# Second block's attentions: two heads of a pair issued side by side, zero-padded remainders of k, and a larger share of projections before the last two groups' suffix sums

## The chip, the core and the metric

The kernel runs on one NeuronCore of a Trainium2 chip. The engines are TensorE (PE, matrix products, with PEld for its weight loads), VectorE (DVE), ScalarE (ACT), GpSimd (POOL) and SyncE (SP, which issues DMAs). The metric is the device time of one execution in microseconds (us): 3792.46 us before, the median of 3 runs (3791.65 to 3796.62).

## The reference, cut to what matters

Two transformer blocks over 512 tokens of width 1024, each with two layers. The change touches only the second block's token mixing, which has three branches per layer, eight heads of 64 values each:

```
for l in range(2):
    h = rmsnorm(x); proj = h @ w_in[l]          # gates, q, k, v of three branches
    y_a = causal_softmax_attention(q_a, k_a, v, 96 ** -0.5)       # "MLA", q and k 96 wide
    y_b = stick_breaking_attention(sb_q, sb_k, sb_v)               # q and k 64 wide
    y_c = silu(r_g) * head_group_norm(retention(r_q, r_k, r_v))    # q and k 64 wide
    x = x + sum_n(sigmoid(gate_n) * (y_n @ w_branch[l, n])) @ w_out[l]
    x = x + square(relu(rmsnorm(x) @ w_up[l])) @ w_down[l]

# stick breaking, per block of 128 keys and the queries at or after them:
z = q @ k.T / 8
between = reverse_cumsum(log_sigmoid(-z)) - log_sigmoid(-z)      # suffix sums over keys
a = where(key < query, exp(log_sigmoid(z) + between), 0);  y = a @ v
```

## The kernel before, in words

All operands are float32. A projection keeps its precision by splitting weight and activation into a rounded part and a remainder and multiplying three times per 128 rows of contraction (`mm3`, lines 330, 332 and 334; `vproj`, lines 1197 to 1199, for the values). These products have 512 (or 256) columns and go through TensorE in one pass. Products of attention weights with values are plain float32; the trace counts two records for each.

`mix` (one call per layer) runs three attentions, each woven with projections: `weave(main, filler)` takes steps of the attention, and after each step issues as many products of the next projections as the number that the step yields (`FILL`, an estimate in us). TensorE works in the order in which it is given instructions; a scheduler orders the other engines' instructions around it.

**MLA** (`mla`). A block is one head and 128 queries. Step i issues the scores of block i (three products, lines 1352 to 1354), then softmax on VectorE and ScalarE, the transposes of block i-2 (line 1370), and the products with v of block i-3 (`mla_av`, line 1382). A head's output takes 64 of the 128 output rows of the array: head 0 of a pair writes rows 0 to 63 of the PSUM tile `yp`, head 1 rows 64 to 127. Blocks run head by head, so neighbouring products write the same half.

**Stick breaking** (`stick`). Eight heads times three groups of key blocks, (2,3), (1) and (0), make 24 groups. Step i issues the scores of group i (`dots`, lines 1323 and 1324), then a chain over VectorE (1428), ScalarE (exp, ln), VectorE (1432), GpSimd (mask, 1437) and VectorE (1439, 1440) that leaves softplus split into two tiles; the suffix sums of group i-2 (`sb_sums`, line 1449), which add to the same PSUM tile; and after a head's third group its products with v (`sb_av`, `av`, line 1291).

**Retention** (`retention`). Two heads of a pair and one key block per step: four score products (lines 1548 and 1550), a product with the decay on VectorE, and the products with v of the step before, which alternate between the two heads already.

For the scores of stick breaking and retention, `pairs` splits q and k into rounded part and remainder. One product over all 128 rows of contraction takes [k rounded; k rounded] with [q rounded; q remainder]; a second, over the 64 rows of the head alone, adds k's remainder times q rounded:

```
nc.tensor.matmul(o, kk[e][:, S], qq[e][:, s * P:], ...)
nc.tensor.matmul(o, kl[half[e], S], qq[e][half[e], s * P:], ...)
```

Tiles come from pools with a fixed number of buffers of 128x512: `ta` (TA = 12) holds attention tiles, `th` (TH = 9) rounded parts and remainders. A new tile waits until an old one is no longer read. In the first block, the neighbourhood attention (`mix` of `na`, line 1000) already issues the products of two heads alternately.

Of the kernel before, what the change touches and what calls it, by code (L numbers as in the profile page):

```python
# [8 lines left out]
F32 = mybir.dt.float32  # L9
F32R = mybir.dt.float32r  # L10
# [3 lines left out]
ALU = mybir.AluOpType  # L14
# [3 lines left out]
P = 128  # L18
# [42 lines left out]
T2 = 16  # L61
TA = 12
TH = 9
TY = 10
NAF = (1.2, 0.55)
NAE = 0.35
FILL = (0.9, 1.9, 1.2)
# [190 lines left out]
class Net:  # L258
# [897 lines left out]
    def mix(self, l, x, xd, xh, xl, pool):  # L1156
# [91 lines left out]
        nc.vector.tensor_tensor(out=t1[64:128], in0=t1[64:128], in1=tk[64:128], op=ALU.add)  # L1248
        kk = []
        for i in range(2):  # L1250
            kh, kl = th(), th()
            self.split(kh[64:128], kl[64:128], t1[64:128])
            kk.append((kh, kl))
        rkv = ta()
# [51 lines left out]

        def pairs(raw):
            q, k = raw
            qq, kk, kl = [th(), th()], [th(), th()], th()
            for e, R in enumerate(half):  # L1310
                nc.scalar.activation(out=qq[e][R], in_=q[R], func=AF.Copy)
                nc.scalar.activation(out=kk[e][R], in_=k[R], func=AF.Copy)
            for e, R in enumerate(half):
                O = half[1 - e]
                nc.vector.tensor_tensor(out=qq[e][O], in0=q[R], in1=qq[e][R].bitcast(F32), op=ALU.subtract)
                nc.vector.tensor_copy(kk[e][O], kk[e][R].bitcast(F32))
                nc.vector.tensor_tensor(out=kl[R], in0=k[R], in1=kk[e][R].bitcast(F32), op=ALU.subtract)
            return qq, kk, kl

        def dots(o, h, s, qk, start):  # L1320
            e, S = h % 2, slice(s * P, s * P + P)
            qq, kk, kl = qk
            nc.tensor.matmul(o, kk[e][:, S], qq[e][:, s * P:], start=start, stop=False, skip_group_check=True)
            nc.tensor.matmul(o, kl[half[e], S], qq[e][half[e], s * P:], start=False, stop=True, skip_group_check=True)

        def next_pair(raw, p):
            if p < 4:
                live["qk", p] = pairs(raw[p])

# [5 lines left out]
        ya = []  # L1335
        blocks = [(h, b) for h in range(8) for b in range(4)]
        live = {}

        def mla_scores(h, b):
            e = h % 2  # L1340
            if b == 0:
                qh, ql = th(), th()
                nc.scalar.activation(out=qh, in_=qraw[h], func=AF.Copy)
                nc.gpsimd.tensor_tensor(out=ql, in0=qraw[h], in1=qh.bitcast(F32), op=ALU.subtract)
                kh, kl = kk[e]
                self.split(kh[:64], kl[:64], kraw[h // 2][64 * e:64 * e + 64])
                live["q"] = (qh, ql)
            (qh, ql), (kh, kl) = live["q"], kk[e]
            w = (b + 1) * P
# [24 lines left out]

        def mla_av(h, b):
            e = h % 2
            if e == 0 and b == 0:
                live["yp"] = yps()
            yp, T = live["yp"], live.pop((h, b))
            c0 = 64 * (h % 4)  # L1380
            for c in range(b + 1):
                nc.tensor.matmul(yp[64 * e:64 * e + 64, b * P:b * P + P], vm[h // 4][:, c, c0:c0 + 64],
                                 T[:, c * P:c * P + P], start=(c == 0), stop=(c == b), skip_group_check=True)
            if e == 1 and b == 3:
                ya.append(out_pair(yp))

        def mla():
            n = len(blocks)
            for i in range(n + 3):
                if i < n:  # L1390
                    mla_scores(*blocks[i])
                    yield FILL[0]
                if 0 <= i - 2 < n:
                    mla_tr(*blocks[i - 2])
                    yield FILL[0]
                if 0 <= i - 3 < n:
                    mla_av(*blocks[i - 3])
                    yield FILL[0]
            for i in range(4):
                self.tap(f"ya{i}", ya[i][0].bitcast(F32))  # L1400
# [13 lines left out]

        self.exp_ln()
        yb = []

# [38 lines left out]

        def sb_av(g):
            h = g["h"]
            p, e = h // 2, h % 2
            if e == 0:  # L1460
                live["yp"] = yps()
            for s in range(4):
                av(live["yp"], e, sv, h, g["a"][s], s)
            if e == 1:
                yb.append(out_pair(live["yp"]))
                self.tap(f"yb{p}", yb[p][0].bitcast(F32))

        def stick():
            groups = []
            next_pair(sb, 0)  # L1470
            for i in range(24 + 3):
                if i < 24:
# [6 lines left out]
                    if h % 2 and j == 0:  # L1479
                        next_pair(sb, h // 2 + 1)  # L1480
                    yield FILL[1]
                if 0 <= i - 2 < 24:
                    sb_sums(groups[i - 2])
                    yield FILL[1]
                if 0 <= i - 3 < 24 and (i - 3) % 3 == 2:
                    sb_av(groups[i - 3])
                    yield FILL[1]

# [46 lines left out]
        def ret_scores(p, s):  # L1535
# [13 lines left out]
            for e, z in enumerate(zs):  # L1549
                nc.tensor.matmul(z, kl[half[e], S], qq[e][half[e], s * P:], start=False, stop=True)  # L1550
            if s == 0:
# [258 lines left out]
```

## Time and profile before

| what | value |
|---|---|
| median of 3 runs | 3792.46 us |
| profiled execution, its own time | 3786.87 us |
| its span, first to last instruction | 3785.1 us |
| mean granted TensorE clock | 0.995 of full speed |
| PE busy | 3717.2 us (98%), 19776 instructions |
| PEld busy | 3011.1 us (80%) |
| DVE busy | 2087.4 us (55%) |
| ACT busy | 1424.6 us (38%) |
| POOL busy | 357.6 us (9%) |

A matmul's recorded duration is longer than what it costs in a stream, since one is in the array while the next enters. What an instruction costs TensorE is read from starts: the start of the next instruction less its own. In layer 0 the MLA stage runs from about 1921 to 2065 us of the span, stick breaking to about 2240, retention from 2252 to 2323; layer 1 repeats them some 960 us later.

### The profile page before, as it was taken

To read this page: it belongs to the slowest core of one execution; us is meant where nothing else is said; L and a number is where in the kernel's file an instruction comes from. 1 tells how busy PE (TensorE), PEld (TensorE's weight loads), DVE (VectorE), ACT (ScalarE), POOL (GpSimd) and SP (SyncE) were. 2 spreads that over 40 slices of the span, in tenths; PEclk is the share of its full clock that TensorE was granted. 3 is DMA by queue.
4 is the path that set the end of the run, shared out by engine and by line. 5 is a ranking of instruction groups with operands and counts; after the bars stand their busy time and mean duration, and the time that the engine had idled before them with its cause. 6 is when DMAs were issued, how large, how long until landed. Compare 5 with 4: busy or idle time off the path is not lost. (4 is left out here: it accounts for less than half of the span.)

```text
span 3785.1 us, 49321 instructions
## 1 busy us (share of the span) xinstructions
PE 3717.2 (98%) x19776; PEld 3011.1 (80%) x19776; DVE 2087.4 (55%) x3320; ACT 1424.6 (38%) x2183; POOL 357.6 (9%) x334
## 2 busy tenths in 40 slices
PE   7999999999999998999999999999999999999998
PEld 6777778888878886888787777888888777688888
DVE  5556653333356775444855775455455576655446
ACT  4333432122344544333545434322234543433223
POOL 2000000000001110000300111211020012112001
PEclk9999999999999999999999999999999999999999
DMA  6343442222222122333322222333332212233333
GB/s 248 126 128 125 140 139 62 62 65 64 62 64 57 50 58 73 95 96 98 111 74 62 67 89 78 118 99 95 101 117 73 65 58 89 80 121 95 100 95 117
DMA packets 122020, 351.86 MB, mean 93 GB/s; under 512 B 30896, under 2 KB 33200, under 8 KB 121792
## 3 DMA queue, kind: packets, MB, share of 16 engines
q1 hardware_dynamic: 87648, 309.11, 26.0%
q10 hardware_dynamic: 32000, 31.67, 2.9%
q0 software_dynamic: 2144, 7.93, 0.5%
q8 instruction: 156, 2.56, 0.3%
q14 instruction: 72, 0.59, 0.0%
HBM read 333.71 MB, written 8.65 MB: 90 GB/s over the span
## 5 line engine op out<-in xcount | busy, mean ns | idle before, releaser
L319 ACT ACTIVATE whi<-wst 128x1024 fp32r<-128x1024 f32 (+3 forms) x503 | 527.3, 1049 | 1404.8 <-PE mm L332 1197.2
L320 DVE TENSOR_TENSOR wlo<-wst,whi 128x1024 fp32r<-128x1024 f32 (+3 forms) x503 | 671.0, 1334 | 330.0 <-ACT whi L319 324.1
L330 PE MATMUL mm<-xh,whi 128*128 128x512 f32 x1664 | 672.0, 404 | 6.0 <-ACT xh L472 3.0
L332 PE MATMUL mm<-xl,whi 128*128 128x512 f32 x1664 | 652.6, 392 | 0.2
L334 PE MATMUL mm<-xh,wlo 128*128 128x512 f32 x1664 | 651.0, 391 | 0.0
L330 PEld LDWEIGHTS mm<-xh,whi 128*128 128x128 f32 x1664 | 313.3, 188 | 90.8 <-issue 26.4
L330 PE MATMUL mm<-ty,whi 128*128 128x512 f32 (+1 forms) x1008 | 382.8, 380 | 0.1
L334 PE MATMUL mm<-ty,wlo 128*128 128x512 f32 (+1 forms) x1008 | 378.9, 376 | 0.0
L334 PEld LDWEIGHTS mm<-xh,wlo 128*128 128x128 f32 x1664 | 313.3, 188 | 69.6 <-issue 2.6
L332 PEld LDWEIGHTS mm<-xl,whi 128*128 128x128 f32 x1664 | 313.9, 189 | 60.3 <-issue 2.3
L330 PE MATMUL mm<-hh,whi 128*128 128x256 f32 (+2 forms) x1176 | 339.5, 352 | 6.4 <-ACT hh L482 2.2
L332 PE MATMUL mm<-hl,whi 128*128 128x512 f32 (+2 forms) x1176 | 332.3, 345 | 2.0 <-DVE hl L486 1.5
L334 PE MATMUL mm<-hh,wlo 128*128 128x512 f32 (+2 forms) x1176 | 329.0, 343 | 0.5 <-DVE wlo L320 0.5
L332 PE MATMUL mm<-ta,whi 128*128 128x512 f32 (+1 forms) x752 | 279.0, 371 | 0.4 <-DVE ta L325 0.4
L330 PEld LDWEIGHTS mm<-hh,whi 128*128 128x128 f32 (+1 forms) x1176 | 188.3, 188 | 65.8 <-issue 34.2
L330 PEld LDWEIGHTS mm<-ty,whi 128*128 128x128 f32 x1008 | 189.7, 188 | 40.6 <-issue 6.2
L334 PEld LDWEIGHTS mm<-ty,wlo 128*128 128x128 f32 x1008 | 189.7, 188 | 35.6 <-issue 1.0
L332 PEld LDWEIGHTS mm<-hl,whi 128*128 128x128 f32 (+1 forms) x1176 | 189.0, 188 | 28.8 <-DVE hl L486 2.0
L334 PEld LDWEIGHTS mm<-hh,wlo 128*128 128x128 f32 (+1 forms) x1176 | 188.5, 188 | 28.9 <-DVE wlo L320 1.0
L332 PEld LDWEIGHTS mm<-ta,whi 128*128 128x128 f32 x752 | 141.7, 188 | 24.9 <-DVE ta L325 0.6
L827 DVE SCALAR_TENSOR_TENSOR x<-mm,mod,x 128x512 f32<-128x512 f32 x52 | 39.0, 750 | 182.2 <-PE mm L334 182.2
L1636 DVE TENSOR_TENSOR x<-x,mm 128x512 f32<-128x512 f32 x56 | 38.5, 687 | 172.1 <-PE mm L334 172.1
(418 smaller groups left out, 6060.3 us busy)
## 6 DMA issues: line engine op xcount, KB each, us to landing
wst<-w_in SPq DMA_DIRECT2D x100, 512.0 KB, 3.5
wst<-ffn_in SPq DMA_DIRECT2D x88, 512.0 KB, 3.5
aw<-ada_w SPq DMA_DIRECT2D x72, 512.0 KB, 4.3
wst<-w_dn SPq DMA_DIRECT2D x70, 512.0 KB, 3.5
wst<-w_up SPq DMA_DIRECT2D x64, 512.0 KB, 3.5
wst<-ffn_out SPq DMA_DIRECT2D x32, 448.0 KB, 3.2
wst<-w_br SPq DMA_DIRECT2D x24, 512.0 KB, 3.5
wst<-gla_qkr SPq DMA_DIRECT2D x16, 512.0 KB, 3.8
```

The lines of the kernel that those rows point to most:

```text
L319: nc.scalar.activation(out=hi[:, :n], in_=st[:, :n], func=AF.Copy)
L320: nc.vector.tensor_tensor(out=lo[:, :n], in0=st[:, :n], in1=hi[:, :n].bitcast(F32), op=ALU.subtract)
L330: nc.tensor.matmul(o, whi, xh, start=first, stop=False)
L332: nc.tensor.matmul(o, whi, xl, start=False, stop=False)
L334: self.after = nc.tensor.matmul(o, wlo, xh, start=False, stop=last)
L827: nc.vector.scalar_tensor_tensor(out=x[:, n, a:b], in0=o[:, :b - a], scalar=gsc, in1=x[:, n, a:b], op0=ALU.mult, op1=ALU.add)
L1636: nc.vector.tensor_tensor(out=x[:, n, :], in0=x[:, n, :], in1=o, op=ALU.add)
```

## The change

1. MLA's blocks are ordered by pair: (pair, query block, head). The products with v wait until both heads' blocks are transposed and are issued for both, alternating between the two halves of `yp`. The q parts of both heads are held at once.
2. Stick breaking's products with v are issued per pair of heads, after the sixth group, alternating in the same way.
3. The remainder of k goes into a tile of four that live on (`kz`), whose other 64 rows hold zeros, written once per layer by GpSimd. The second score product of stick breaking and retention now runs over all 128 rows. MLA's own k tiles use the same four buffers before.
4. Steps 24 and 25 of stick breaking, which have no scores to issue, yield 4.0 each to the projections, ahead of the suffix sums of groups 22 and 23.
5. TA from 12 to 15, TH from 9 to 8.

```diff
-TA = 12
-TH = 9
+TA = 15
+TH = 8
...
-        kk = []
-        for i in range(2):
-            kh, kl = th(), th()
+        kz = [tag("kz", 4, F32R) for _ in range(4)]
+        kk = [kz[0:2], kz[2:4]]
+        for kh, kl in kk:
             self.split(kh[64:128], kl[64:128], t1[64:128])
...
-        def pairs(raw):
+        def pairs(raw, par):
-            qq, kk, kl = [th(), th()], [th(), th()], th()
+            qq, kk, kl = [th(), th()], [th(), th()], kz[2 * par:2 * par + 2]
...
-                nc.vector.tensor_tensor(out=kl[R], in0=k[R], in1=kk[e][R].bitcast(F32), op=ALU.subtract)
+                nc.vector.tensor_tensor(out=kl[e][R], in0=k[R], in1=kk[e][R].bitcast(F32), op=ALU.subtract)
...
-            nc.tensor.matmul(o, kl[half[e], S], qq[e][half[e], s * P:], start=False, stop=True, skip_group_check=True)
+            nc.tensor.matmul(o, kl[e][:, S], qq[e][:, s * P:], start=False, stop=True, skip_group_check=True)
...
-        blocks = [(h, b) for h in range(8) for b in range(4)]
+        blocks = [(2 * p + e, b) for p in range(4) for b in range(4) for e in range(2)]
...
-        def mla_av(h, b):
+        def mla_av(p, b):
+            yp, Ts = live["yp"], [live.pop((2 * p + e, b)) for e in range(2)]
             for c in range(b + 1):
+                for e, T in enumerate(Ts):
+                    c0 = 64 * (2 * p % 4 + e)
+                    nc.tensor.matmul(yp[64 * e:64 * e + 64, b * P:b * P + P], vm[p // 2][:, c, c0:c0 + 64],
+                                     T[:, c * P:c * P + P], start=(c == 0), stop=(c == b), skip_group_check=True)
...
-                if 0 <= i - 3 < n:
-                    mla_av(*blocks[i - 3])
-                    yield FILL[0]
+                if i >= 4 and i % 2 == 0:
+                    mla_av(blocks[i - 4][0] // 2, blocks[i - 4][1])
+                    yield 2 * FILL[0]
...
+        for i, z in enumerate(kz):
+            nc.gpsimd.memset(z[half[1 - i % 2]].bitcast(F32), 0.0)
...
+        def sb_av(p, gs):
+            yp = yps()
             for s in range(4):
+                for e, g in enumerate(gs):
+                    av(yp, e, sv, 2 * p + e, g["a"][s], s)
...
+                elif i < 26:
+                    yield 4.0
...
-                if 0 <= i - 3 < 24 and (i - 3) % 3 == 2:
-                    sb_av(groups[i - 3])
-                    yield FILL[1]
+                if 0 <= i - 3 < 24 and (i - 3) % 6 == 5:
+                    sb_av((i - 3) // 6, (groups[i - 6], groups[i - 3]))
+                    yield 2 * FILL[1]
...
-                nc.tensor.matmul(z, kl[half[e], S], qq[e][half[e], s * P:], start=False, stop=True)
+                nc.tensor.matmul(z, kl[e][:, S], qq[e][:, s * P:], start=False, stop=True)
```

How this moves TensorE's instructions, at two places. First, in MLA of layer 0 before the change, a block's products with v (line 1382, here one key block of one head) between projections (lines 330, 332, 334), with the scores of the next block (1352 to 1354) behind:

```order
L334 MATMUL mm<-xh,wlo 128x512
L1382 MATMUL yp<-ta,v 64x128
L330 MATMUL mm<-xh,whi 128x512
L332 MATMUL mm<-xl,whi 128x512
L334 MATMUL mm<-xh,wlo 128x512
L330 MATMUL mm<-xh,whi 128x512
L332 MATMUL mm<-xl,whi 128x512
L334 MATMUL mm<-xh,wlo 128x512
L1352 MATMUL ma<-th 128x128
```

The same stage after the change, where the line is 1381 and x4 counts two key blocks of two heads:

```order
L1381 MATMUL yp<-ta,v 64x128 x4
L330 MATMUL mm<-xh,whi 128x512
L332 MATMUL mm<-xl,whi 128x512
L334 MATMUL mm<-xh,wlo 128x512
L330 MATMUL mm<-xh,whi 128x512
L332 MATMUL mm<-xl,whi 128x512
L334 MATMUL mm<-xh,wlo 128x512
L330 MATMUL mm<-xh,whi 128x512
L332 MATMUL mm<-xl,whi 128x512
L334 MATMUL mm<-xh,wlo 128x512
L1351 MATMUL ma<-kz,th 128x512
```

The products with v stand in half as many places, each with both heads' products and more projections behind it. Second, TensorE in stick breaking of layer 0 before the change: one head's products with v (line 1291), one per key block:

```order
L334 MATMUL mm<-ty,wlo 128x512
L1291 MATMUL yp<-ta,v 64x512
L1291 MATMUL yp<-ta,v 64x384
L1291 MATMUL yp<-ta,v 64x256
L1291 MATMUL yp<-ta,v 64x128
L330 MATMUL mm<-ty,whi 128x512
```

After the change (line 1290):

```order
L334 MATMUL mm<-ty,wlo 128x512
L1290 MATMUL yp<-ta,v 64x512 x2
L1290 MATMUL yp<-ta,v 64x384 x2
L1290 MATMUL yp<-ta,v 64x256 x2
L1290 MATMUL yp<-ta,v 64x128 x2
L330 MATMUL mm<-ty,whi 128x512
```

Both heads' products now stand at one place, alternating, at the end of the pair; the place at the end of the first head is gone.

## Rows read from the trace of the kernel before

**Rows 1.** Windows, layer 0's MLA and stick breaking: us, busy PE, PEld, DVE, ACT, POOL, clock, DMA
```profile
1921.00:2065.00 144.00, 144.00 (x823) 115.35 (x821) 78.99 (x211) 70.79 (x152) 8.41 (x6) 1.00 0.20 63
2065.00:2240.00 175.00, 174.88 (x865) 134.40 (x865) 125.12 (x232) 74.15 (x121) 26.55 (x38) 1.00 0.24 73
```

**Rows 2.** Timeline, PE, MLA: start us, us, engine, line, operation, tiles
```profile
1961.31 1.09 PE L1382 MATMUL yp<-ta,v 128*64 128x128 f32 x8
1962.33 0.50 PE L1352 MATMUL ma<-th 128*128 128x512 f32 x1
...
1994.11 0.40 PE L334 MATMUL mm<-xh,wlo 128*128 128x512 f32 x1
1994.43 0.87 PE L1382 MATMUL yp<-ta,v 128*64 128x128 f32 x6
1995.23 0.50 PE L330 MATMUL mm<-xh,whi 128*128 128x512 f32 x1
1995.57 0.40 PE L332 MATMUL mm<-xl,whi 128*128 128x512 f32 x1
1995.81 0.39 PE L334 MATMUL mm<-xh,wlo 128*128 128x512 f32 x1
```

**Rows 3.** Timeline, PE and PEld, first block's neighbourhood attention, heads alternating
```profile
1200.59 1.09 PE L1000 MATMUL po<-T,v 128*64 128x128 f32 x16
1201.61 0.39 PE L924 MATMUL mm<-whi,hh 128*128 128x256 f32 x1
...
1200.59 0.85 PEld L1000 LDWEIGHTS po<-T,v 128*64 128x64 f32 x16
```

**Rows 4.** Timeline, PE, stick breaking, one head's products with v
```profile
2094.94 2.37 PE L1291 MATMUL yp<-ta,v 128*64 128x512 f32 x8
2097.23 0.50 PE L330 MATMUL mm<-ty,whi 128*128 128x512 f32 x1
```

**Rows 5.** Timeline, PE, retention, two heads' products with v
```profile
2257.14 1.08 PE L1291 MATMUL yp<-ta,v 128*64 128x512 f32 x4
2258.15 0.50 PE L330 MATMUL mm<-xh,whi 128*128 128x512 f32 x1
```

**Rows 6.** Timeline, PE, stick breaking, first score product and next projection, groups (0), (2,3)
```profile
2071.21 0.40 PE L1323 MATMUL ma<-th 128*128 128x512 f32 x1
...
2071.96 0.50 PE L330 MATMUL mm<-xh,whi 128*128 128x512 f32 x1
...
2099.42 0.28 PE L1323 MATMUL ma<-th 128*128 128x256 f32 x1
...
2100.45 0.50 PE L330 MATMUL mm<-ty,whi 128*128 128x512 f32 x1
```

**Rows 7.** Timeline, PE, retention, first of four score products and next projection
```profile
2252.27 0.62 PE L1548 MATMUL ma<-th 128*128 128x512 f32 x2
...
2253.24 0.50 PE L330 MATMUL mm<-xh,whi 128*128 128x512 f32 x1
```

**Rows 8.** Timeline, stick breaking: chain of group 0; split and sums of groups 21, 23
```profile
2065.09 0.56 DVE L1428 TENSOR_SCALAR ta<-ma 128x384 uint32<-128x384 uint32 x1 [0.23 <-PE ma L1324]
...
2071.57 0.56 DVE L1440 TENSOR_TENSOR ta<-ta 128x384 fp32r<-128x384 f32 x1
...
2074.13 0.80 PE L1449 MATMUL ma<-ta,rc 128*128 128x128 f32 x6
...
2220.14 0.56 DVE L1440 TENSOR_TENSOR ta<-ta 128x384 fp32r<-128x384 f32 x1
...
2225.99 0.80 PE L1449 MATMUL ma<-ta,rc 128*128 128x128 f32 x6
...
2233.66 0.68 DVE L1440 TENSOR_TENSOR ta<-ta 128x512 fp32r<-128x512 f32 x1
...
2236.20 1.37 PE L1449 MATMUL ma<-ta,rc 128*128 128x512 f32 x8
```

More of the change, by code (lines that the diff above doesn't have):

```diff
@@ L1248, in mix @@
         nc.vector.tensor_tensor(out=t1[64:128], in0=t1[64:128], in1=tk[64:128], op=ALU.add)
-        kk = []
-        for i in range(2):
-            kh, kl = th(), th()
+        kz = [tag("kz", 4, F32R) for _ in range(4)]
+        kk = [kz[0:2], kz[2:4]]
+        for kh, kl in kk:
             self.split(kh[64:128], kl[64:128], t1[64:128])
-            kk.append((kh, kl))
         rkv = ta()
@@ L1323, in dots @@
             nc.tensor.matmul(o, kk[e][:, S], qq[e][:, s * P:], start=start, stop=False, skip_group_check=True)
-            nc.tensor.matmul(o, kl[half[e], S], qq[e][half[e], s * P:], start=False, stop=True, skip_group_check=True)
+            nc.tensor.matmul(o, kl[e][:, S], qq[e][:, s * P:], start=False, stop=True, skip_group_check=True)
         def next_pair(raw, p):
             if p < 4:
-                live["qk", p] = pairs(raw[p])
+                live["qk", p] = pairs(raw[p], p % 2)
         def out_pair(src):
@@ L1346, in mla_scores @@
                 self.split(kh[:64], kl[:64], kraw[h // 2][64 * e:64 * e + 64])
-                live["q"] = (qh, ql)
-            (qh, ql), (kh, kl) = live["q"], kk[e]
+                live["q", e] = (qh, ql)
+            (qh, ql), (kh, kl) = live["q", e], kk[e]
             w = (b + 1) * P
@@ L1373, in mla_tr @@
             live[h, b] = T
-        def mla_av(h, b):
-            e = h % 2
-            if e == 0 and b == 0:
+        def mla_av(p, b):
+            if b == 0:
                 live["yp"] = yps()
-            yp, T = live["yp"], live.pop((h, b))
-            c0 = 64 * (h % 4)
+            yp, Ts = live["yp"], [live.pop((2 * p + e, b)) for e in range(2)]
             for c in range(b + 1):
-                nc.tensor.matmul(yp[64 * e:64 * e + 64, b * P:b * P + P], vm[h // 4][:, c, c0:c0 + 64],
-                                 T[:, c * P:c * P + P], start=(c == 0), stop=(c == b), skip_group_check=True)
-            if e == 1 and b == 3:
+                for e, T in enumerate(Ts):
+                    c0 = 64 * (2 * p % 4 + e)
+                    nc.tensor.matmul(yp[64 * e:64 * e + 64, b * P:b * P + P], vm[p // 2][:, c, c0:c0 + 64],
+                                     T[:, c * P:c * P + P], start=(c == 0), stop=(c == b), skip_group_check=True)
+            if b == 3:
                 ya.append(out_pair(yp))
@@ L1388, in mla @@
             n = len(blocks)
-            for i in range(n + 3):
+            for i in range(n + 4):
                 if i < n:
@@ L1455, in sb_sums @@
                 g["a"][s] = l1[:, o:o + NL - s * P]
[L1457 to L1461, printed above, removed]
+        def sb_av(p, gs):
+            yp = yps()
             for s in range(4):
[L1463 to L1466, printed above, removed]
+                for e, g in enumerate(gs):
+                    av(yp, e, sv, 2 * p + e, g["a"][s], s)
+            yb.append(out_pair(yp))
+            self.tap(f"yb{p}", yb[p][0].bitcast(F32))
         def stick():
```

## The prediction

> **What bounds the kernel now.** I read the profile in this order: the table of busy shares, the busy time of each engine in the stages that change, then TensorE's timeline from start to start around every kind of product that the change touches, and last how long before the suffix sums their operands are ready. In both stages of [rows 1] TensorE is busy for the whole window (144.00 of 144 us, 174.88 of 175) at the full clock, the 2.4 GHz level, so what a product costs TensorE is what it costs the kernel. VectorE is the next engine, with 125.12 of 175 us in stick breaking.
>
> The second thing to see is that some products cost far more than their columns. A projection product of 512 columns starts 0.24 us before the next (1995.57 to 1995.81) [rows 2]; I use 0.23, the step that repeats through the stage within 0.01. The products with v fill half of the array's output rows. Three of them, for one head, take 0.80 us (1994.43 to 1995.23), four take 1.02 (1961.31 to 1962.33): 0.22 each and 0.14 once per burst [rows 2]. Going in costs 0.09 more (0.32 instead of 0.23 ahead of 1994.43), coming out 0.11 more (0.34 instead of 0.23 after 1995.23) [rows 2]. So a burst of n products costs 0.22 n + 0.34.
>
> **Term 1, MLA's products with v, -28.5 us.** Two layers, eight heads and four blocks make 64 bursts with 160 products: 160 x 0.22 + 64 x 0.34 = 57.0 us. The change pairs the products of two heads, which write different halves. What a pair costs is shown by the first block's neighbourhood attention, which already alternates: 16 records, eight products, take 1.02 us (1200.59 to 1201.61) [rows 3], what four take for one head. So 80 pairs in 32 bursts cost 80 x 0.22 + 32 x 0.34 = 28.5.
>
> A rule speaks against this. The Trainium skill ("TensorE: Matmul & The Clock Gate", Part 3, on packing small matmuls) lets a weight load run beside a product in flight only where the two use different row groups; both heads here use all rows, so each load would stand in line with the other head's product. The trace disagrees: with the 16 loads busy for 0.85 us, the whole burst of [rows 3] lasts only 1.02. By the row term 1 is 28.5 us, by the rule it is 10.9 (second rival).
>
> **Term 2, stick breaking's products with v, -19.6.** One head's four products, of 512 to 128 columns, take 2.29 us [rows 4], with 0.20 in and out 2.49; 16 heads cost 39.8. Two heads' products of 512 columns, alternating in retention, take 1.01 (2257.14 to 2258.15) [rows 5]; less the 0.14 per burst that is 0.87 per 512 columns. A pair's 1280 columns cost 0.87 x 2.5 + 0.14 + 0.20 = 2.52, eight pairs 20.2.
>
> **Term 3, stick breaking's scores, -23.0.** Each product over the half array sits between two over the whole one, and each turn costs. Group (0) takes 0.75 us for two products of 512 columns (2071.21 to 2071.96), and 0.10 on coming out [rows 6]; two whole-array products of that width take 0.46 [rows 2]. Gain 0.39. Group (2,3) takes 1.03 for four (2099.42 to 2100.45) and 0.11 [rows 6]; at half the width or less, four cost at most 4 x 0.12, by half of the 0.23. Gain 0.66. Group (1), with one turn like (0), I take at 0.39. That is 1.44 per head, 23.0 for 16. No row shows the zero-padded product itself; the bounds are the price of a whole-array product and, if the padding gained nothing, zero.
>
> **Term 4, retention's scores, -6.** Two whole and two half products of 512 columns take 0.97 us (2252.27 to 2253.24) [rows 7] and 0.10 out; four whole ones 0.92. Gain 0.15, over 32 steps 4.8. The narrower three widths pay the same turns on less work, but two heads share a turn, so the 0.39 of term 3 (12.5 us) is the other end. I take 6, near its own row. Products with v alternate there already and stay.
>
> **Sum on TensorE:** 28.5 + 19.6 + 23.0 + 6 = 77.1 us.
>
> **What it may cost.** In stick breaking the chain of a group hides behind the projections between its scores and its sums. Group 0's splits end at 2071.57 + 0.56 = 2072.13 and its sums start at 2074.13, 2.0 us later; group 21's are 5.3 ahead (2220.70 to 2225.99), group 23's 1.9 (2234.34 to 2236.20) [rows 8]. Between a group's scores and its sums TensorE now saves about 0.4 to 0.7 us for each score group passed. The first groups lose up to half of their 2.0 us, so I allow 1 us per layer: 2 us; bounds zero and 4 (the whole 2.0 per layer). The last two get the 2 x 4.0 us of projections that ran after them: group 23 gains cover, and what stands ahead of retention shrinks by as much. That costs nothing if the first retention pair is split in time; its q and k are projected long before. If that cover were too short, the nearest row for such a chain is 7.0 us (2065.09 to 2072.13) [rows 8] per layer, 14 in all.
>
> MLA's k tiles are now rewritten after the last block of one pair for the first of the next, where there used to be another head's four blocks between. The PE order leaves projections, transposes and a v burst in between, which I count as enough: zero; the nearest row for a late operand, 2.0 us [rows 8], times six turns is 12. The four memsets of GpSimd per layer wait for MLA's last scores; behind them in its queue stands only the mask of group 0. VectorE's subtraction into `kz` needs no free `th` tile any more, so a small gain is possible too: zero, within 2 us either way. The same holds for the scheduler's other choices with 15 and 8 tiles. The number of VectorE, ScalarE and DMA instructions in these stages stays, but for the memsets and the split of which tile takes them.
>
> So the change is 77.1 - 2 = 75 us. The profiled execution lasts 3786.87 us (span 3785.1 and 1.8 around it), and would come to 3712; the median of the runs is 5.6 above it, and the same step from 3792.46 gives **3717 us**.
>
> **Rivals.**
> - *VectorE becomes the bound of stick breaking.* For: it is busy 125.12 of 175 us [rows 1], and terms 2 and 3 take 21 us per layer out of the window, which brings it to 81%, in order and with waits. Against: its results lie 5.3 us ahead of the sums late in the stage [rows 8], more than the first groups have. Price: if VectorE gets no faster at all, TensorE gains only that lead, 5.3 of 21.3 us per layer; 32 us are lost: 3749.
> - *The pairs don't overlap* (the change doesn't do what it says; the rule of the skill named above would bring this about). MLA then costs 160 x 0.22 + 32 x 0.34 = 46.1 instead of 57.0, a gain of 10.9; stick breaking eight bursts of 2 x 2.15 + 0.34 = 4.64, 37.1 instead of 39.8. Terms 1 and 2 give 13.6 instead of 48.1: 3752. Against: [rows 3, 5] show the overlap, once with one bank and 128 columns, once with the same `yp` tile.
> - *Slower, by the `ta` tiles.* A pair's six tiles of weights now live until both heads are done, so up to nine such tiles and six split tiles are held: all 15. If the first group of the next pair finds no tile until the pair's products with v have run, its whole chain, 7.0 us [rows 8], and the wait for the burst ahead stand open at each of eight pair turns. From 9.4 us per turn the 75 are gone; at 9.9 it is 3796. Against: 12 tiles were as tight (six and six) at every head, and TensorE lost nothing there.
> - *Cover gone at stage boundaries* (the 14 and 12 us above): 3731 to 3743.
>
> **How the numbers follow.** Forecast 0.80, by itself 3708 to 3727 (term 4 up to 12.5 and a gain of 2 with waits of 1; or waits of 12). VectorE as the bound 0.09, boundaries 0.05, no overlap 0.03, slower 0.03. The range 3708 to 3738 holds the forecast and part of the boundary and VectorE cases; below 2 in 10 is left out. Within 0.2% (7.6 us, what a measurement of this kernel can tell from no change) no case has its centre; I give 0.02 for mixtures of the last three. Faster 0.95, slower 0.03.
>
> **What would show it right or wrong.** In the profile after: bursts of MLA's products with v at 0.36 to 1.02 us for two heads; one pair's products in stick breaking at about 2.3 us; steps of 0.23 us for both score products at 512 columns, without a long one behind; both stages with TensorE still busy throughout; stick breaking about 21 us and MLA about 14 us shorter per layer. It is wrong if TensorE's timeline shows holes ahead of the suffix sums or the transposes, if VectorE's share in stick breaking goes over 90%, or if a pair's burst takes 4 us.

## The result, and the profile after

The changed kernel takes 3752.39 us (median of 4 runs, 3751.86 to 3753.64) beside 3792.06 us for the kernel before in the same comparison: a ratio of 0.9897, 95% interval 0.9884 to 0.9909. That is 40 us faster. The forecast was 75 us, and 3752 lies 14 us above the top of its range. The profiled execution lasts 3752.21 us, its span 3750.4.

Three windows of the changed kernel in layer 0 answer to [rows 1]: MLA, the stick breaking from its first score product to the last suffix sums, and from there to retention's first score product. The columns are those of [rows 1].

```profile
1925.20:2054.10 128.90, 127.87 (x803) 106.03 (x801) 76.91 (x210) 69.42 (x149) 7.51 (x8) 1.00 0.22 69
2054.10:2215.70 161.60, 158.90 (x876) 133.62 (x876) 119.27 (x225) 73.35 (x123) 27.37 (x38) 0.99 0.25 75
2215.70:2238.20 22.50, 14.19 (x52) 9.20 (x52) 10.96 (x17) 2.14 (x3) 3.59 (x2) 0.77 0.31 94
```

MLA is shorter and nearly full. The stick breaking's last stretch is neither: TensorE is busy 14.19 of 22.50 us at a granted clock of 0.77. The same stretches, from TensorE's starts in layer 0 of each kernel's profile (us; "last sums" is the first product of group 23's sums, and retention is from its first to its last score product; the other kernels are those of the experiments below):

| kernel | MLA | stick breaking to last sums | to retention | sum of the two | retention |
|---|---|---|---|---|---|
| before | 140.9 | 172.3 | 16.1 | 188.4 | 65.7 |
| after | 128.9 | 161.6 | 22.5 | 184.1 | 63.2 |
| mla_pair_only | 128.2 | 172.1 | 16.1 | 188.2 | 65.9 |
| sb_pair_only | 140.9 | 165.3 | 20.1 | 185.4 | 65.7 |
| kz_only | 141.1 | 164.3 | 17.5 | 181.8 | 63.2 |
| yield_only | 140.9 | 180.5 | 11.8 | 192.3 | 65.7 |
| no_yield | 128.9 | 160.2 | 20.3 | 180.5 | 63.3 |
| rg_last | 128.9 | 164.4 | 17.3 | 181.7 | 63.3 |
| exch_out | 128.9 | 157.1 | 9.9 | 167.0 | 63.2 |
| exch_sp | 128.9 | 157.1 | 15.6 | 172.7 | 63.2 |
| exch_sp_rot_pool | 128.9 | 158.1 | 12.0 | 170.1 | 63.2 |
| early_act | 128.9 | 170.4 | 9.9 | 180.3 | 63.2 |

MLA gave 12.0 us a layer and retention 2.5. The stick breaking gave only 4.3, of 21 expected. Layer 1 reads alike (12.0, 2.5 and 3.6). Over both layers that is 36.9 us; the spans of the two profiled executions differ by 34.7.

TensorE's timeline of the changed kernel, answering [rows 2, 4, 6, 7]: MLA's four products for each of two heads (x16) and what follows; a pair's products in stick breaking; the scores of a group (2,3); retention's first scores.

```profile
1959.76 1.09 PE L1381 MATMUL yp<-ta,v 128*64 128x128 f32 x16
1960.79 0.39 PE L1197 MATMUL mm<-whi,xh 128*128 128x256 f32 x1
...
2182.41 2.38 PE L1290 MATMUL yp<-ta,v 128*64 128x512 f32 x16
2184.72 0.50 PE L330 MATMUL mm<-xh,whi 128*128 128x512 f32 x1
...
2188.24 0.28 PE L1322 MATMUL ma<-th 128*128 128x256 f32 x1
...
2188.65 0.45 PE L330 MATMUL mm<-xh,whi 128*128 128x512 f32 x1
...
2238.24 0.62 PE L1548 MATMUL ma<-th 128*128 128x512 f32 x2
...
2239.16 0.40 PE L330 MATMUL mm<-xh,whi 128*128 128x512 f32 x1
```

So the products cost what was forecast: 1.03 us for two heads' four products in MLA (1.02), 2.31 for a pair in stick breaking (2.32), 0.41 for the four of a group (2,3) (at most 0.48), 0.92 for retention's four (0.92).

What went wrong stands at the end of the stage. TensorE, from group 23's sums (L1450) to the last pair's products with v (L1290):

```profile
2215.75 1.76 PE L1450 MATMUL ma<-ta,rc 128*128 128x512 f32 x8
2217.34 0.44 PE L330 MATMUL mm<-xh,whi 128*128 128x512 f32 x1
...
2219.56 1.07 PE L1290 MATMUL yp<-ta,v 128*64 128x512 f32 x2
2228.82 4.53 PE L1290 MATMUL yp<-ta,v 128*64 128x512 f32 x14 [8.19 <-DVE ta L1455]
2233.28 0.80 PE L330 MATMUL mm<-xh,whi 128*128 128x512 f32 x1
```

The pair's burst lasts from 2219.56 to 2233.28, 13.72 us in place of 2.31. It waits 8.19 us for VectorE's L1455, the masking of the last weights. ScalarE and VectorE in the same time (ACTq is ScalarE's issue of transfers):

```profile
2220.24 2.46 ACTq L1514 DMA_DIRECT2D tf<-s  x4
2222.81 0.60 ACT L301 ACTIVATE ta<-ma 128x512 f32<-128x512 f32 x1 [8.71 <-DMA tf<-s]
```
```profile
2215.52 0.68 DVE L1441 TENSOR_TENSOR ta<-ta 128x512 fp32r<-128x512 f32 x1
...
2219.53 0.68 DVE L1207 TENSOR_TENSOR s<-mm,rsb 128x512 f32<-128x512 f32 x1
...
2226.01 0.69 DVE L1516 TENSOR_TENSOR s<-s,cosr 128x512 f32<-128x512 f32 x1 [4.67 <-DMA tf<-s]
2227.86 0.69 DVE L1517 TENSOR_TENSOR s<-s,tf 128x512 f32<-128x512 f32 x1 [1.15 <-POOL tf L1515]
2228.47 0.29 DVE L1455 COPY_PREDICATED ta<-rc,con_mask_sb 128x128 f32<-128x128 uint32 x1
```

Read it in order. Group 23's second split (L1441) ends at 2216.20, when its sums have begun at 2215.75: the lead of 1.9 us in [rows 8] is gone, and that alone costs little. The sums are through at 2217.34, so its exponential (L301, from `ma`) could start then. But ahead of it in ScalarE's queue stand four copies of retention's rotary step (L1514, the exchange of 32-row blocks), and these wait for the tile that VectorE's L1207 scales, finished at 2220.21. They are issued from 2220.24 for 2.46 us, and only then, 5.5 us late, the exponential runs. It ends at 2223.41. Now L1455 stands in VectorE's queue behind L1516, which waits for those copies to land, and L1517, which waits for GpSimd: 2228.47, another 5.1 us late. None of these rotary instructions belongs to the work that TensorE waits for.

The clock makes it worse. The granted clock around the hole is the figure behind the five engines' busy times:

```profile
2219.50:2228.80 9.30, 1.13 (x3) 0.19 (x2) 3.47 (x7) 1.54 (x2) 1.77 (x1) 0.78 0.41 137
2228.80:2233.30 4.50, 4.48 (x15) 2.36 (x15) 1.68 (x2) 0.00 (x0) 0.00 (x0) 0.50 0.49 127
2233.30:2238.20 4.90, 4.90 (x19) 4.03 (x19) 2.08 (x3) 0.60 (x1) 1.81 (x1) 0.84 0.13 49
```

After the idle stretch the remaining seven products run wholly at 0.50, the 1.2 GHz level: 4.46 us (2228.82 to 2233.28) for what takes about 1.9 at the full one (an estimate: the whole pair's 2.31 less one of two 512-column products, 0.87 / 2). The same queueing makes a smaller hole earlier in the stage. ScalarE's exponential of another group's sums waits 1.45 us for a copy's issue, so the PSUM tile that the next scores want comes free late, and the next 5 us have a granted clock of 0.68:

```profile
2174.79 0.49 ACT L301 ACTIVATE ta<-ma 128x384 f32<-128x384 f32 x1 [1.45 <-DMA tf<-s]
```
```profile
2175.34 0.50 PE L1322 MATMUL ma<-th 128*128 128x512 f32 x1 [1.90 <-ACT ta L301]
```
```profile
2175.00:2180.00 5.00, 4.66 (x17) 3.94 (x17) 2.27 (x5) 1.75 (x3) 1.67 (x1) 0.68 0.32 113
```

TensorE's whole list of waits names both, over two layers (total, times, longest); neither line is in that of before:

```profile
PE yp L1290 <- DVE ta L1455: 16.6, 2, 8.4
...
PE ma L1322 <- ACT ta L301: 4.5, 4, 1.9
```

### The profile page after: what moved, and what is told of

Read it like the earlier page. It is cut to its first block, busy times and chain, and to the rows that moved or that the text cites. A ratio compares the mean times of both kernels' runs of the same rounds, so it can differ in the third digit from the quotient of the medians.

```text
span 3750.4 us, 49324 instructions
## 1 busy us (share of the span) xinstructions
PE 3655.5 (97%) x19776; PEld 2996.6 (80%) x19776; DVE 2074.2 (55%) x3320; ACT 1421.1 (38%) x2183; POOL 365.0 (10%) x342
## 4 chain that ended last, share of the span: by engine, by line
PE 43%; DVE 3%; DMA 2%; ACT 1%; POOL 1%; issue 1%; ACTq 0%; DVEq 0%; POOLq 0%; SPq 0%
PE mm L330 12%; PE mm L334 12%; PE mm L332 12%; DMA tf<-s 1%; PE yp L1290 1%; PE mm L1197 1%; PE mm L1199 1%; PE mm L1198 1%; PE ma L1450 1%; PE yp L1381 1%; POOL tf L1515 1%; DVE wlo L320 0%; ACTq L1514 0%; ACT ta L301 0%; PE ma L1369 0%
## 5 line engine op out<-in xcount | busy, mean ns | idle before, releaser
L334 PEld LDWEIGHTS mm<-hh,wlo 128*128 128x128 f32 (+1 forms) x1176 | 188.4, 188 | 28.9 <-DVE wlo L320 1.0
L1636 DVE TENSOR_TENSOR x<-x,mm 128x512 f32<-128x512 f32 x56 | 38.5, 687 | 172.1 <-PE mm L334 172.1
```

Source lines behind the costliest of these rows:

```text
L334: self.after = nc.tensor.matmul(o, wlo, xh, start=False, stop=last)
L1636: nc.vector.tensor_tensor(out=x[:, n, :], in0=x[:, n, :], in1=o, op=ALU.add)
```

## The experiments

Theory A is the one just told: in-order queues of ScalarE and VectorE, tied together by the exchange copies. Theory B says that group 23's own chain is too long for what is left beside it. The first four runs were made to find the place, before this was clear.

**no_yield**: the changed kernel without the larger share of projections.
```
-                elif i < 26:
-                    yield 4.0
```


> The changed kernel without the two yields of 4.0, so that nine projection products instead of 27 stand before the sums of groups 22 and 23 and 54 instead of 18 behind the last products with v. Theory (the yields put a rope piece, with its exchange by DMA, between the last sums and the last products with v, and these wait in order behind it): the hole of 9 us and the half clock behind it, about 12 us per layer, go; 3728 us (3722 to 3734). Rival (VectorE is simply late because TensorE's stage became shorter): the same lateness meets fewer projections; the hole stays or grows, 3748 to 3765 us.


Measured: 3750.52 us, ratio 0.990 (0.988 to 0.9921), no different from the changed kernel and in the rival's range. The hole only moved, from the product to the sums (layer 0; the profiled execution took 3741.70 us):
```profile
2211.24 2.98 PE L1450 MATMUL ma<-ta,rc 128*128 128x512 f32 x8 [7.30 <-DVE ta L1440]
```
So taking the larger share away cures nothing. It does not follow that VectorE is simply late: group 23's step of VectorE (L1433) stands here behind the rotary multiplication, which waited 1.83 us for a landing, and with the copies on SyncE's queue (exch_sp_no_yield below) 4.1 of the 7.3 us are left.

**rg_last**: the changed kernel with the gate projections `rg` of pairs 1 to 3 last, so that plain projections would lie at the end.
```
-                o = yield from gproj(22 + p)
-                rg.append(...)
+                for r in ((), (), (0,), (1, 2, 3))[p]:
+                    o = yield from gproj(22 + r)
+                    rg.append(...)
```


> The changed kernel with its yields, but the projections of the retention gate for pairs 1 to 3, which have no exchange by DMA, come last in the filler, after all of retention's q and k; the number of products before and behind each place stays. Theory (it is the exchange that stands in the way): the hole goes, 3729 us (3723 to 3736). Rival (too few projections are left behind the last products with v, of whatever kind): the hole stays, 3748 to 3756 us.


Measured: 3744.41 us, ratio 0.988 (0.9863 to 0.9898). Between the two. The waits for L1455 remain (6.3 us in two), and ScalarE's exponential still waits 6.63 us for copies: the filler runs by TensorE's order, so the rotary pieces still came late.

**yield_only**: the kernel before with the larger share.
```
+                elif i < 26:
+                    yield 4.0
```


> The kernel before with nothing but the two yields of 4.0. Theory: the rope piece comes between the last sums and the last products with v here too, a hole of 4 to 12 us per layer, 3800 to 3816 us. Rival (it takes the shorter stage to make VectorE late): no change, 3789 to 3795 us.


Measured: 3795.88 us, ratio 1.0019 (1.0007 to 1.0031): a loss of some 7 us, just above the rival's range. The hole of the theory is there in both layers, only smaller, and it is made by the copies (ScalarE, TensorE and the window behind the wait, layer 0):
```profile
2248.32 2.44 ACTq L1516 DMA_DIRECT2D tf<-s  x4
2250.86 0.60 ACT L301 ACTIVATE ta<-ma 128x512 f32<-128x512 f32 x1 [5.68 <-DMA tf<-s]
```
```profile
2245.51 1.37 PE L1449 MATMUL ma<-ta,rc 128*128 128x512 f32 x8
2251.85 3.98 PE L1291 MATMUL yp<-ta,v 128*64 128x512 f32 x8 [2.17 <-DVE ta L1454]
```
```profile
2251.85:2255.76 3.91, 3.91 (x8) 1.49 (x8) 0.69 (x1) 0.00 (x0) 1.70 (x1) 0.58 0.25 96
```
The sums are through by 2246.72, but the exponential waits until four copies are issued. TensorE waits 2.17 us for the mask, and the head's four products then take 3.91 us at a granted clock of 0.58, where [rows 4] has 2.29. These two make 3.8 us a layer, which is what the stage lost (192.3 beside 188.4). In the kernel before, the same copies are issued behind the last exponential:
```profile
2237.66 0.60 ACT L301 ACTIVATE ta<-ma 128x512 f32<-128x512 f32 x1 [2.83 <-PE ma L1449]
...
2242.10 2.46 ACTq L1514 DMA_DIRECT2D tf<-s  x4
```
So it is the larger share, the fourth part of the change, that brings a rotary piece ahead of the last exponential.

**kz_only**: the kernel before with the zero-padded key remainders (and 8 `th` tiles).
```
-                nc.tensor.matmul(o, kl[half[e], S], qq[e][half[e], s * P:], ...)
+                nc.tensor.matmul(o, kl[e][:, S], qq[e][:, s * P:], ...)
```


> The kernel before with the zero-padded remainder of k alone (both score products over 128 rows, in stick breaking and retention), TH 8. By terms 3 and 4 of the prediction TensorE's work falls by 29 us and nothing else moves: 3763 us (3759 to 3768). Rival (VectorE holds stick breaking already at this length): half or less of it, 3776 us or more.


Measured: 3768.85 us, ratio 0.9944 (0.9928 to 0.996): 20 us of the 29 of terms 3 and 4, just above the first expectation. Retention gave its 2.5 us a layer, the stick breaking 6.6 of 11.5 in layer 0. TensorE waits 2.3 us for L1455 and 1.9 for L301 there, the two instructions for which it waits in the changed kernel too.

**exch_out**: the changed kernel without the exchange copies.
```
-                    for b in range(4):
-                        nc.scalar.dma_start(out=sw[32 * b:32 * b + 32], in_=raw[...])
-                    nc.gpsimd.tensor_tensor(out=sw, in0=sw, in1=self.sinr, op=ALU.mult)
+                    nc.gpsimd.tensor_tensor(out=sw, in0=raw, in1=self.sinr, op=ALU.mult)
```


> The changed kernel without the exchange of 32-row blocks in the retention's rotary step: the four ScalarE-issued copies per tile (L1514) are left out and GpSimd multiplies the unexchanged tile, so that part of the computation differs; all else stands. Theory A (the missing gain went into ScalarE's and VectorE's in-order queues in the last 20 us of stick breaking, where group 23's exponential stands behind the issue of these copies, which wait for their own data, and L1455 behind the multiplication that waits for the copies to land): the hole of 8 us ahead of the last pair product goes, and with it the stretch at half granted clock behind it. 3752 less two layers of 10.9 us of waits is 3730; with the 5 us a layer of clock it is 3720: 3718 to 3733. Theory B (group 23's own chain of ScalarE, VectorE and GpSimd steps is too long for the TensorE work that is left there, whoever else stands in the queues): 3742 to 3752, with the hole in the same place, now ended by a step of the chain.


Measured: 3720.93 us, ratio 0.9815 (0.9796 to 0.9834), as theory A had it. The windows, as for the changed kernel above:
```profile
1924.10:2053.00 128.90, 127.87 (x803) 106.03 (x801) 76.95 (x210) 69.38 (x149) 7.49 (x8) 1.00 0.23 69
2053.00:2210.10 157.10, 156.47 (x876) 132.58 (x876) 125.57 (x235) 73.34 (x123) 30.37 (x39) 1.00 0.24 71
2210.10:2220.00 9.90, 9.90 (x52) 7.22 (x51) 4.74 (x7) 2.14 (x3) 2.29 (x1) 1.00 0.32 101
```
TensorE is full to the end at the full clock, with the same VectorE work but for the copies' waits. The kernel computes something else and so is a bound, not a remedy. The stick breaking is 21.4 us shorter than before (188.4 to 167.0); the forecast's terms say 21.3.

**exch_sp**: the changed kernel with the copies issued by SyncE.
```
-                        nc.scalar.dma_start(out=sw[...], in_=raw[...])
+                        nc.sync.dma_start(out=sw[...], in_=raw[...])
```


> The changed kernel with the same exchange copies issued from SyncE's queue in place of ScalarE's; the computation is whole. Theory A1 (what costs is that ScalarE stands still while an issue waits for its data): ScalarE's exponentials run on, the hole shrinks to what VectorE waits for the landing of the copies (4.7 us at the one, less the 2.4 us of issue): 3725 to 3738. Theory A2 (what costs is VectorE, which waits for the transfer whoever issues it, and SyncE's queue is itself behind weight loads): 3745 to 3756, with VectorE's wait of L1516 as long as before. Theory B (the chain of group 23): 3745 to 3752.


Measured: 3728.37 us, ratio 0.9838 (0.9818 to 0.9857), 24 us below the changed kernel: theory A1. Of the two delays, ScalarE's is gone, and VectorE's is still there (ScalarE, VectorE and TensorE):
```profile
2211.71 0.60 ACT L301 ACTIVATE ta<-ma 128x512 f32<-128x512 f32 x1 [3.58 <-PE ma L1450]
```
```profile
2215.13 0.69 DVE L1516 TENSOR_TENSOR s<-s,cosr 128x512 f32<-128x512 f32 x1 [2.89 <-DMA tf<-s]
2216.97 0.69 DVE L1517 TENSOR_TENSOR s<-s,tf 128x512 f32<-128x512 f32 x1 [1.15 <-POOL tf L1515]
2217.58 0.30 DVE L1455 COPY_PREDICATED ta<-rc,con_mask_sb 128x128 f32<-128x128 uint32 x1
```
```profile
2217.93 3.79 PE L1290 MATMUL yp<-ta,v 128*64 128x512 f32 x14 [3.19 <-DVE ta L1455]
```
The exponential now waits for nothing but the sums. L1455 still stands behind the rotary multiplication, 5.3 us after the exponential's end at 2212.31.

**mla_pair_only**: the kernel before with MLA's part alone (its diff is MLA's hunks and the `kz` tiles).
```
+        blocks = [(2 * p + e, b) for p in range(4) for b in range(4) for e in range(2)]
...
+            for c in range(b + 1):
+                for e, T in enumerate(Ts):
...
```


> The kernel before with the change's first part alone: MLA's heads in pairs (block order, both heads' products with v interleaved), which needs the padded key remainders' tiles; the stick breaking, its scores and the retention stay as before. If the first term stands by itself, the kernel before (3789 in the last call's runs) loses 24 us (the 12 us a layer by which MLA's stage shrank in the changed kernel) to 28.5 (as predicted): 3760 to 3766. Rival: part of what MLA's stage lost there is filler work moved into the stick breaking, so that alone it gives 10 to 18 us: 3771 to 3779.


Measured: 3765.03 us, ratio 0.9936 (0.9917 to 0.9955), 24 to 27 us by the comparison's medians: term 1 stands by itself, and 12.7 us a layer are seen in its stage.

**sb_pair_only**: the kernel before with the stick breaking's pairs alone, 15 `ta` tiles.
```
-                if 0 <= i - 3 < 24 and (i - 3) % 3 == 2:
-                    sb_av(groups[i - 3])
+                if 0 <= i - 3 < 24 and (i - 3) % 6 == 5:
+                    sb_av((i - 3) // 6, (groups[i - 6], groups[i - 3]))
...
```


> The kernel before with the second part alone: the stick-breaking products with v for two heads at once, every sixth group, and nothing else (no padded key remainder, no larger share of projections). If the second term is free as predicted: 3789 less 19.6 is 3769 to 3771. Theory A and B both say that the end of the stage cannot use all of it, since the last pair's product now wants groups 18 to 23 all at once: of 9.8 us a layer 3 to 7 remain: 3775 to 3783. Rival of no gain: 3786 to 3792.


Measured: 3784.69 us, ratio 0.9982 (0.997 to 0.9993): some 7 us of 19.6, the low end of the 3 to 7 us a layer that theories A and B both had (the time lies 1.7 us above their range, but the kernel before took 3792.34 in this comparison, not 3789). In its stage in layer 0 it is 3.0 us. Here TensorE waits for group 23's chain ahead of its sums, since no larger share covers it:
```profile
2241.12 0.80 PE L1449 MATMUL ma<-ta,rc 128*128 128x512 f32 x1 [4.00 <-DVE ta L1439]
```
```profile
2238.41 1.78 POOL L1512 TENSOR_TENSOR tf<-tf,sinr 128x512 f32<-128x512 f32 x1 [8.57 <-DMA tf<-s]
2240.15 0.45 POOL L1437 TENSOR_TENSOR ta<-ta,con_mask_sb 128x128 f32<-128x128 f32 x1
```
That wait is not the chain's own alone: GpSimd's mask (L1437) could start when VectorE's L1432 ended at 2237.03, and started 3.1 us later behind the rotary product L1512, which waited for copies to land.

**before_exch_sp**: the kernel before with exch_sp's edit, the control.


> The kernel before with one edit: the exchange copies of the retention's rotary step are issued from SyncE's queue in place of ScalarE's. Theory A (the copies only cost where the stick breaking's end has no cover left): TensorE waited nowhere for this stage's end in the kernel before (172.3 and 16.1 us a layer, no wait of TensorE in the list), so nothing is to be had: 3785 to 3793. Rival (moving the issues to SyncE is worth its 24 us to any kernel, and has nothing to do with the change): 3764 to 3775.


Measured: 3789.19 us, ratio 0.9998 (0.9989 to 1.0007). The edit that gives the changed kernel 24 us gives the kernel before nothing. The copies stood in ScalarE's queue there too, but the last exponential ran ahead of them (the rows under yield_only), and TensorE waited for nothing: its list of waits has no line in this stage.

**exch_sp_rg_last**: exch_sp's and rg_last's edits together.


> The changed kernel with the exchange copies on SyncE's queue, and with the retention's gate projections of pairs 1 to 3 at the very end of the stage's filler, so that plain projections and not rotary pieces lie under the last groups. With the copies on SyncE alone 3728 was measured, with a 3.2 us wait of TensorE for L1455 a layer left; without copies 3721. Theory A1: what is left is VectorE's wait for the landing of late copies, which now lies earlier: 3719 to 3725. Rival (the pieces still come late, since TensorE runs ahead of its feeders, or SyncE's queue delivers late): 3726 to 3733.


Measured: 3737.22 us, ratio 0.9859 (0.9844 to 0.9874), above both expectations. The rotary multiplication is again ahead of L1455 (VectorE waits 2.70 us for a landing), and now two pair products wait for L1455, 4.6 us in all (1.2 and 3.4); why the earlier of them waits is not shown. Moving plain projections to the end did not take the rotary pieces off the critical places.

**exch_sp_no_yield**: exch_sp's and no_yield's edits together.


> The changed kernel with the exchange copies on SyncE's queue and without the two larger shares of projections ahead of the last two groups' sums. Theory A1 with a chain of its own (group 23's steps last 5 to 6 us and want about two projections ahead of its sums and one ahead of the product): a wait of 2 to 6 us a layer appears at L1450: 3730 to 3740. Rival (the larger shares were never needed, the hole came from the copies alone): 3718 to 3727.


Measured: 3734.20 us, ratio 0.9854 (0.9838 to 0.987), as theory A1 has it with a chain of its own: a wait of its own appears,
```profile
PE ma L1450 <- DVE ta L1440: 4.1, 1, 4.1
```
Without the larger share this wait is open; with it (exch_sp) it is not there. So the larger share does cover group 23's chain, once the copies are out of ScalarE's queue; the two intervals overlap, and the wait is the better evidence.

**exch_pool**: the copies issued by GpSimd (`nc.gpsimd.dma_start`).


> The changed kernel with the exchange copies issued from GpSimd's queue. Theory A1 (any engine that holds a link of a group's chain and issues these copies in order is late by their waits): GpSimd's mask L1438 now stands behind issues, VectorE's L1440 waits for it, and the time is 3738 to 3756. Rival (only ScalarE is hit, by the length of its own issue): 3724 to 3732, as with SyncE.


Measured: 3754.47 us, ratio 0.9911 (0.9896 to 0.9926), no better than ScalarE's queue and in A1's range, but not by A1's way. Two pair products wait (TensorE; then ScalarE and VectorE ahead of the second):
```profile
2194.74 4.50 PE L1290 MATMUL yp<-ta,v 128*64 128x512 f32 x14 [3.54 <-DVE ta L1455]
...
2239.50 4.53 PE L1290 MATMUL yp<-ta,v 128*64 128x512 f32 x14 [4.46 <-DVE ta L1455]
```
```profile
2232.01 0.60 ACT L301 ACTIVATE ta<-ma 128x512 f32<-128x512 f32 x1 [5.19 <-PE ma L1450]
```
```profile
2236.64 1.80 DVE L1516 TENSOR_TENSOR s<-s,cosr 128x512 f32<-128x512 f32 x1 [5.44 <-DMA tf<-s]
...
2239.15 0.30 DVE L1455 COPY_PREDICATED ta<-rc,con_mask_sb 128x128 f32<-128x128 uint32 x1
```
GpSimd's mask L1438 was expected to be late behind the issues; at the end of the stage it is not, for there it waits for VectorE. The last exponential runs on time, behind its sums alone. What is late is L1455, behind VectorE's wait for a landing, as with SyncE's queue but longer (5.44 us beside 2.89; the median from issue to landing is 3.3 us beside 2.0). So this run does not show that an engine with a link of the chain must not issue, only that GpSimd's queue is no remedy here.

**exch_sp_rot_pool**: exch_sp, and L1516 and L1517 on GpSimd.
```
-                    nc.vector.tensor_tensor(out=raw, in0=raw, in1=self.cosr, op=ALU.mult)
-                    nc.vector.tensor_tensor(out=raw, in0=raw, in1=sw, op=ALU.add)
+                    nc.gpsimd.tensor_tensor(out=raw, in0=raw, in1=self.cosr, op=ALU.mult)
+                    nc.gpsimd.tensor_tensor(out=raw, in0=raw, in1=sw, op=ALU.add)
```


> The changed kernel with the exchange copies on SyncE's queue and the two steps behind them (the product with the cosine and the sum, L1516 and L1517) on GpSimd in place of VectorE, so that no instruction of VectorE waits for a copy. Theory A1 (what is left between 3728 with the copies on SyncE and 3721 without them is L1455 behind VectorE's wait for a landing, 3.2 us of TensorE a layer and the clock behind it): 3718 to 3724, no wait of TensorE for L1455. Rival (GpSimd's own longer steps delay the masks L1438 of groups 22 and 23, or the rotated tiles come too late for the splits): 3727 to 3740.


Measured: 3726.02 us, ratio 0.983 (0.9814 to 0.9847), just above A1's 3724. TensorE has no wait for L1455 left, and the end of the stage shrinks from 15.6 to 12.0 us in layer 0 and to 10.4 in layer 1, where exch_out has 9.9. The middle of the stage grows by 1.0 (158.1 beside 157.1). It is the lowest time of the whole computation, though its interval overlaps exch_sp's.

**early_act** and **early_sp**: the rotary pieces of pairs 0 to 2 ahead of the last three up projections, pair 3's ahead of the gate projections; the copies on ScalarE's and on SyncE's queue.
```
             for c in range(KD):
+                if c >= 5:
+                    yield from rope(c - 5)
                 u = yield from up(0, ya, c, wb)
...
```


> The changed kernel with the rotary pieces of pairs 0 to 2 ahead of the last three up projections, pair 3's ahead of the gate projections and these last; the copies stay in ScalarE's queue. If it is the place of the copies in the program that costs, not the queue as such, most of the hole goes: 3719 to 3732. Rivals: the wait moves with pair 3's pieces, which still come late (3735 to 3748); or the pieces now wait for tiles that the stick breaking's pairs hold, and TensorE waits in mid-stage (3740 to 3760).

> The same order of pieces with the copies in SyncE's queue. If both place and queue matter, this is at least as good as SyncE's queue alone: 3717 to 3726. Rivals as for the kernel with ScalarE's queue: 3728 to 3740 where pair 3's pieces still meet the last product, above that where tiles are short in mid-stage.


Measured: 3741.23 us (ratio 0.9874, 0.9856 to 0.9892) and 3741.06 (0.9879, 0.9862 to 0.9896). Out of the end, the copies cost nothing on either queue: both ends last 9.9 us, as in exch_out. But the stage to the last sums is 170.4 and 171.2 us, for a reason that no expectation named: the value projections, now late, wait for ScalarE and for a weight's split (early_act, layer 0):
```profile
PE mm L1197 <- ACT v L1202: 5.1, 3, 3.1
PE mm L1198 <- DVE wlo L320: 2.5, 1, 2.5
```
So it takes both, copies late in the program and ScalarE's (or GpSimd's) queue, to open the whole of the hole (with late copies on SyncE's queue 3.2 us of TensorE's wait are left). What early copies would gain with the value projections in their old place was not run.

## Why the prediction was wrong

*What bounds the kernel, and the price of each product:* right. TensorE was the bound, and the bursts that answer to [rows 2, 4, 6, 7] came out within 0.1 us.

*Term 1 (28.5 us):* 24.0 in the stage, 2.25 us a layer short. In layer 0 the bursts take 12.5 us after and 22.2 before, a gain of 9.7 where 11.0 was forecast: two of the 16 bursts are broken in two by other products, and one of these holds a wait of about 0.6 us for ScalarE. The turns in and out still cost 0.2 a burst, and 15 bursts fell away (33 to 18, where 32 to 16 was counted): 3.0 of 3.2. TensorE waits another 0.4 us for ScalarE in this stage, where it waited for nothing before. That leaves 0.3 us a layer open. The Trainium skill's rule that a weight load runs beside a product only with other row groups ("TensorE: Matmul & The Clock Gate", Part 3) is not borne out here either: 1.03 and 2.31 us are the times of two heads side by side.

*Terms 2 and 3 (42.6):* right on TensorE, as exch_out shows with 2 x 21.4 us, and not to be had in the changed kernel, which got 4.3 and 3.6 of it.

*Term 4 (6):* 5.0.

*The step that failed is "What it may cost", 2 us.* It measured cover only from a group's splits to its own sums [rows 8], and said of the end that it "costs nothing if the first retention pair is split in time". It looked neither at the way from the sums to the product with v (exponential, mask) nor at what else stands in ScalarE's and VectorE's queues there. It counted the instructions of those engines as unchanged, which they are, and so as free. Nor did it look at what the projections moved ahead of the last sums bring with them: copies that ScalarE issues. The larger share alone costs the kernel before some 7 us (yield_only). In the changed kernel the price was 17.1 us a layer (184.1 beside exch_out's 167.0): 11.4 at the last product (13.72 less 2.31, of which 8.19 is the wait and 2.6 the half clock), some 2 in the hole at 2175, and about 2.4 in the slower clock behind both (5 us at 0.68, 4.9 at 0.84); somewhat over 1 us is not placed. The allowed 14 us for both layers together ("cover gone at stage boundaries") named the end of the stage, but for retention's first pair, and neither the size nor the cause.

*The rivals.* VectorE as the bound gave 3749, near the measured 3752 by chance; it is not what happened: VectorE is busy 130.2 of 184.1 us, 71%, and in exch_out 130.3 of 167.0, 78%, with TensorE full. It was late because it waited in order, not because it was full. Pairs without overlap, also at 3752, are excluded by the bursts. The `ta` tiles cost nothing visible in TensorE's list of waits; no run tried them alone.

*What would show it wrong* named holes ahead of the sums and the transposes. The hole was one step further, ahead of the products with v.

Shown by runs: the copies cause the loss (exch_out), through ScalarE's queue for the most part (exch_sp), through VectorE's for the rest of the wait (exch_sp_rot_pool). In the kernel before they cost nothing (before_exch_sp), until the larger share puts them ahead of the last exponential (yield_only). Open: 0.3 us a layer of MLA, and how much of group 23's chain is its own where the copies are not taken away (sb_pair_only, no_yield).

## What to carry to other kernels

Where the busiest engine gets faster, list for the last operands of each stage every instruction that stands ahead of them in their engines' queues, those of other stages' work above all, and what each of these waits for. A transfer that waits for data is better in the queue of an engine without a link of the chain (SyncE's here, 24 us; GpSimd's gave nothing), and an operation that waits for its landing is better kept off the engine of the last link (moved from VectorE to GpSimd, which holds only an earlier one, it left no wait for L1455, though the 2 us gained are within the noise). A busy share of 71% says nothing about that.

## What the runs showed of the hardware

A wait of TensorE cost more than itself here: after 8.19 us of it the clock stayed at 0.50 for 4.5 us and averaged 0.84 over the next 4.9, and after only 1.90 us it averaged 0.68 over 5 us. That the clock falls to 1.2 GHz on idling is in the Trainium skill ("TensorE: Matmul & The Clock Gate", Part 1); the trace agrees.

The same copies, four to a tile, cost 24 us more on ScalarE's queue than on SyncE's in the changed kernel, and nothing more in the kernel before. The Trainium skill ("DMA: Bandwidth & Descriptors", "Issuing engines are not separate DMA queues") says that issuing from several engines only saves the sequencer's time to start a transfer, usually little beside the transfer. Here that time was 2.46 us for four copies, and what counted was that the issue waits, in ScalarE's order, for the tile that it reads: ScalarE stood idle for 8.71 us ahead of its exponential, 5.5 of them after the sums were through.
